# GpSimd subtracts for 17 units of the input projection, not 36; latent attention as two runs of four heads

## The chip, the cores and the metric

The kernel runs on one core of one Trainium2 chip. A core has five engines that work side by side, each through its own queue in order: TensorE (PE; its weight loads are shown as PEld), VectorE (DVE), ScalarE (ACT), GpSimd (POOL) and SyncE (SP, which issues the large loads). [...] The metric is the device time of one execution in microseconds (us); lower is better.

## The reference, cut to what matters

Two model blocks follow each other on 256 tokens of width 1024, in float32. The first block has a retention layer and a latent-attention layer, each with a feed-forward network (FFN) behind it; the second has a token mixer with a wide input projection, and a mixture of experts. The two pieces that the change touches:

```python
# latent attention, 8 heads, query blocks of 128 (16 meta tokens stand before the 256)
q = (cq @ w_q_b).reshape(B, L, 8, 128 + 64)
for qb in range(L // 128):
    sc = einsum('bqhd,bkhd->bhqk', q[:, s:e], k[:, :e]);  p = softmax(where(mask, sc, -1e30))
    outs.append(einsum('bhqk,bkhd->bqhd', p, v[:, :e]))
h = h + concat(outs) @ w_o                       # all heads

# token mixer of the second block
h = rms_norm(x, norm1_w) * (1 + sc1) + sh1
proj = h @ w_in                                   # 1024 x 5640: qa, ka, va, qkv_b, z, b, a, gates
```

## The kernel before, in words

Activations lie transposed, features on 128 partitions and tokens along the row. A float32 product is made of three products of fp32r operands: every weight and every activation x is cut into a high part `hi` (ACT rounds x to fp32r, L162) and a low part `lo` = x - hi (L168), and `mm3` (L306) issues hi·xh, hi·xl and lo·xh into one PSUM bank.

Weights come in chunks of 16 tiles of 128x128 (1 MB) that SP loads ahead into 5 buffers; a **unit** is 8 tiles, 128x1024, and is cut by one ACT and one subtraction. `Weights.ahead` (L151) keeps three units cut ahead of the products, in 4 buffers of `hi` and 4 of `lo`. The subtraction of a unit is written one unit later than its `hi`. `W.aside` (L257) names the units whose subtraction is put on GpSimd instead of DVE: here the 36 units from the first one that holds tiles of `win`, the input projection of the token mixer. That first unit, number 0 in this text, holds the last four tiles of the FFN's second product and the first four of `win`.

The order of the work is the order in which the Python code runs; nothing reorders it. `gemm` (L362) walks through column groups, each of two PSUM banks, and calls `tick` after every tile; every fourth (or ninth) tick takes one step of each generator in `sides` (L330): small work that is threaded between the products. `evac` reads a finished bank. `later` keeps small DVE instructions for the next ticks. `drain` and `until` take side steps with no products between them.

**Latent attention** (L817 to L951). `mla_proj(g)` makes keys, values and queries of heads 4g to 4g+3. It ends with two column groups that give `qn`, two heads each. The heads go through `pipeline` (L918): `scores` (two heads at a time on PE; mask, softmax on DVE and ACT), a free step, `trans` (five transposes on PE, copies `pt` and `ptm` on ACT) and `av` (four products on PE, then `oh`, `ol` by ACT and DVE, shown as `xbh`, `xbl`). At each time t the pipeline takes av of head t-3, trans of t-2 and scores of t. One pipeline walks through all 8 heads, and scores of heads 4 to 7 are let in when `ready` is set, after all of `mla_proj(1)`. Then `until` (L940) steps on until four heads are out, `mo` multiplies them by the first half of w_o, `drain` ends the other four, and `mo` takes the second half.

**The input projection** (L973 to L1480). The FFN of the first block ends with `evac_f1` (L958): hx is added up (L937), ACT makes the square, the scaled x and `xbh`, DVE makes `xbl` and two sums of squares. Products: `ba` (8 tiles), `qa2` and `ka2` (32 each, on xbh/xbl, 258 columns), then `va2` (32, weights moving), `dn` (96), `z` (32), the gates `ga`, `gb`. While ba, qa2 and ka2 run, DVE and ACT make the eight row blocks of the normed input (`modulated`, L1000: L1004, L1005 on DVE, L1006 on ACT, L1008 on DVE), read out qm and km (L1139), and prepare decays (`decays`, L1071; its cols at L1091 go into a small PE product at L1096). `va2` is not begun before `modulated` is through (L1164). `lev` (L1039) and the bias tables (`m_bias`, L1153) are loaded from GpSimd's queue.

Of the kernel before, what the change touches and what calls it, by code (L numbers as in the profile page):

```python
# [18 lines left out]
SEQ = 256  # L19
# [220 lines left out]
def body(ctx, tc, I, O):  # L240
    nc = tc.nc
    V, A, P = nc.vector, nc.scalar, nc.tensor
# [11 lines left out]

    W = Weights(nc, rawp, splitp, I["wd"], I["we"], order, split, 5, 4)
    first_win = min(i for i, t in enumerate(order) if t and t[0] == "win") // UNIT
    W.aside = lambda v: first_win <= v < first_win + 36  # L257

    hx = keep.tile([128, KD, T], F32, name="hx")
    vec = const.tile([128, VEC["n"]], F32, name="vec")  # L260
# [37 lines left out]
    def bank(pool, name):  # L298
        return pool.tile([128, 512], F32, tag=name, name=name)
# [6 lines left out]
    def mm3(ps, w, x, first, last):  # L306
        P.matmul(ps, w[0], x[0], start=first, stop=False)  # L307
        P.matmul(ps, w[0], x[1], start=False, stop=False)  # L308
        P.matmul(ps, w[1], x[0], start=False, stop=last)  # L309

    def mm3t(ps, x, w, first, last):
        P.matmul(ps, x[0], w[0], start=first, stop=False)
        P.matmul(ps, x[0], w[1], start=False, stop=False)
        P.matmul(ps, x[1], w[0], start=False, stop=last)

    def split_to(hi, lo, src):
        A.activation(hi, src, AF.Copy)  # L317
        V.tensor_sub(lo, src, hi.bitcast(F32))  # L318
# [9 lines left out]
    sides = []  # L328

    def side_step():  # L330
        for g in list(sides):
            try:
                next(g)
            except StopIteration:
                sides.remove(g)

    def drain(gen):
        while gen in sides:
            side_step()

    def until(done):
        while not done():
            side_step()
# [7 lines left out]
    def flush():  # L351
        while pend:
            pend.pop(0)()

    def tick(every=4):
        quantum[0] += 1
        if pend and quantum[0] % 2 == 0:
            pend.pop(0)()
        if quantum[0] % every == 0:
            side_step()  # L360

    def gemm(mat, ks, ngroups, g, x, n, evac, after_first=None, every=4, hold=False):  # L362

        for gi in range(ngroups):
            pss = [bank(mmp, "mm") for _ in range(g)]
            for kk in range(ks):
                for j in range(g):
                    mm3(pss[j][:, :n], W.take(mat), x(kk), kk == 0, kk == ks - 1)
                    tick(every)
            flush()  # L370
            if gi == 0 and after_first:
                after_first()
                if not hold:
                    flush()
            for j in range(g):
                evac(gi * g + j, pss[j][:, :n])
        if not hold:
            flush()
# [71 lines left out]
    o = VEC["mix0"][0]  # L450
# [39 lines left out]
    def rope(put, pss, cs, n):  # L490

        c, s = cs[:, 0], cs[:, 1]
        for j, (a, b, op) in enumerate(((c, s, OP.subtract), (s, c, OP.add))):
            def half(j=j, a=a, b=b, op=op):
                t = tmp.tile([128, 2, T], F32, tag="rt", name="rt")
                V.tensor_mul(t[:, 0, :n], pss[0], a)
                V.tensor_mul(t[:, 1, :n], pss[1], b)
                put(j, op, t[:, 0, :n], t[:, 1, :n])
            later(half)
# [160 lines left out]
    def ffn_open(which):  # L660
        return dict(x=xbuf(which), acc=keep.tile([128, T], F32, tag="acc", name="facc"))
# [57 lines left out]
    la = {}  # L719
# [85 lines left out]
    G = {}  # L805

    def normq():
        r = la["rq"] = row_scale(qacc, SEQ, 1.0 / 768, 1e-6, "rq", lat)
        V.tensor_scalar(r, r, 192.0 ** -0.5, None, op0=OP.mult)
        cs = la["qcs"] = lat.tile([128, 2, SEQ], F32, name="qcs")  # L810
        for j in range(2):
            V.tensor_mul(cs[:, j], rope_m[:, j], r)

    cpair = lambda k: (ch[:, k], cl[:, k])
    qpair = lambda k: (qh[:, k, :SEQ], ql[:, k, :SEQ])

    def mla_proj(g):  # L817
        d = G[g] = {}
        kn = d["kn"] = pb.tile([128, 4, T], F32, tag="kn", name="kn")
        gemm("kvb", 4, 2, 2, cpair, T,  # L820
             lambda j, ps: V.tensor_mul(kn[:, j], ps, la["rc"]))
        pss = [bank(mmp, "mm") for _ in range(2)]
        pm = bank(sdp, "side")
        i = W.pos
        for k in range(4):
            w = W.take("kvb", 4)
            for j in range(2):
                o = 128 * j
                mm3t(pss[j], (ch[:, k, o:o + 128], cl[:, k, o:o + 128]), w, k == 0, k == 3)
                tick()  # L830
        for k in range(4):
            P.matmul(pm[32 * k:32 * k + 32], c32[:, k], W.raw_at(i + 4 * k, 4), start=True, stop=True,
                     tile_position=(0, 32 * k))
        v = d["v"] = pb.tile([128, 2, 512], F32, tag="lv", name="lv")
        for j in range(2):
            A.activation(v[:, j], pss[j], AF.Copy, scale=la["rccol"][:, j:j + 1])
        mp = lat.tile([128, 512], F32, tag="lmp", name="lmp")
        A.activation(mp, pm, AF.Copy)
        if g == 0:
            normq()  # L840
        qr = d["qr"] = pb.tile([128, 2, SEQ], F32, tag="qr", name="qr")
        got = []

        def put(i, op, a, b):

            for h in range(4):
                o = 64 * (h % 2) + 32 * i
                V.tensor_tensor(qr[o:o + 32, h // 2], a[32 * h:32 * h + 32], b[32 * h:32 * h + 32], op=op)

        def evac(j, ps):  # L850
            got.append(ps)
            if j == 1:
                rope(put, got, la["qcs"], SEQ)
        gemm("qb", 6, 1, 2, qpair, SEQ, evac)
        pv = bank(sdp, "side")
        P.matmul(pv[0:16], gsel, mp, start=True, stop=True)
        vm = d["vm"] = pb.tile([16, 512], F32, tag="lvm", name="lvm")
        A.activation(vm, pv[0:16], AF.Copy)
        qn = d["qn"] = pb.tile([128, 4, SEQ], F32, tag="qn", name="qn")
        gemm("qb", 6, 2, 2, qpair, SEQ, lambda j, ps: V.tensor_mul(qn[:, j], ps, la["rq"]))  # L860
        d["ready"] = True

    H = {}

# [41 lines left out]
    def av(h):  # L906
        g, i = divmod(h, 4)
        d, e = G[g], H.pop(h)
        c = slice(128 * i, 128 * i + 128)
        po = bank(sdp, "side")  # L910
        P.matmul(po[:, 0:256], d["v"][:, 0, c], e["t"][:, 0:256], start=True, stop=False)
        P.matmul(po[:, 128:256], d["v"][:, 1, c], e["t"][:, 256:384], start=False, stop=False)
        P.matmul(po[:, 64:128], d["v"][0:16, 1, c], e["tm"][:, 64:128], start=False, stop=False)
        P.matmul(po[:, 192:256], d["vm"][:, c], e["tm"][:, 192:256], start=False, stop=True)
        split_to(oh[:, h], ol[:, h], po[:, 0:256])
        la["heads"] = h + 1

    def pipeline(stages, n, ready=None, lead=0):  # L918
        m = len(stages)
        for t in range(n + m - 1):  # L920
            if t == 2:
                for _ in range(lead):
                    yield
            for si in reversed(range(m)):
                if 0 <= t - si < n and stages[si]:
                    while ready and not ready(si, t - si):
                        yield
                    stages[si](t - si)
                    yield

    mla_proj(0)
    mside = pipeline([scores, None, trans, av], 8, lambda si, h: si or "ready" in G.get(h // 4, {}))
    sides.append(mside)
    mla_proj(1)

    def add_x(j, ps):
        V.tensor_add(hx[:, j, XS], hx[:, j, XS], ps)  # L937

    opair = lambda k: (oh[:, k], ol[:, k])
    until(lambda: la.get("heads", 0) >= 4)  # L940
    gemm("mo", 4, 4, 2, opair, SEQ, add_x)
    drain(mside)
    F1 = ffn_open("a")

    def evac_l1(j, ps):
# [8 lines left out]
    o = VEC["fin"][0]  # L954
# [1015 lines left out]
    g = [st[:, 3, t:t + 1] for t in range(2)]  # L1970
# [150 lines left out]
```

## Time and profile before

| what | value |
|---|---|
| time, median of 3 runs | 1294.42 us (1292.28 to 1295.43) |
| the profiled execution: its own time, its span | 1295.5 us, 1293.7 us |
| PE busy | 1223.9 us, 95% |
| DVE, ACT, POOL busy | 799.5, 597.4, 99.9 us |
| mean granted TensorE clock | 0.973 |
| latent attention, projections to the last head | about 450 to 579 us |
| ba to va2 | 778 to 840 us |
| dn, z, ga, gb | 840 to about 955 us |

How to read it: matmuls overlap each other, so a busy PE is an upper bound, and PE is waiting only where a row names idle time before an instruction. [...] Idle time on the other engines costs nothing by itself. From about 1050 us on the expert weights come in at some 415 GB/s; SP starts to issue them when the token mixer's buffers are given up.

### The profile page before, as it was taken

Reading aid. Unit: us, or ns where it says so; the run is one execution under the profiler, and the core shown is the slowest. Engines: PE = TensorE matmul, PEld = TensorE weight load, DVE = VectorE, ACT = ScalarE, POOL = GpSimd, SP = SyncE. Lnnn points to the kernel's source line nnn. Section 1 sums busy time; section 2 is a strip of 40 time slices with the busy share of each in tenths; the row PEclk is TensorE's granted clock in tenths of the full one; section 3 lists DMA queues with packets and bytes.
Section 4 is the critical chain, followed back from the end, with each engine's and each line's share of the span. In section 5 each row is a group of like instructions: output and inputs, shape, how many; then the busy total and the mean of one; then the engine's idle time right before and its main releaser. Section 6 shows DMA issues by size and latency. Waiting matters only on the chain. (4 is left out here: it accounts for less than half of the span.)

```text
span 1293.7 us, 24265 instructions
## 1 busy us (share of the span) xinstructions
PE 1223.9 (95%) x9994; PEld 1055.7 (82%) x9994; DVE 799.5 (62%) x1404; ACT 597.4 (46%) x1017; POOL 99.9 (8%) x59
## 2 busy tenths in 40 slices
PE   8999999999999999999999998799999998777896
PEld 7889798999999998889999998599789974232453
DVE  7465665987777887649877887646645743121223
ACT  5544546644445564556544554667334531010123
POOL 0000000000000000000000025667100000000000
PEclk9999999999999999989999998899999999897898
DMA  8433434476657854414766784444114779999992
GB/s 299 177 144 130 144 126 175 152 264 225 228 193 296 314 176 183 164 66 166 291 228 233 271 296 157 151 158 164 67 67 176 317 288 414 417 418 418 417 418 76
DMA packets 47362, 293.08 MB, mean 227 GB/s; under 512 B 6384, under 2 KB 7296, under 8 KB 15360
## 3 DMA queue, kind: packets, MB, share of 16 engines
q1 hardware_dynamic: 45216, 286.52, 58.5%
q0 software_dynamic: 2016, 4.76, 1.0%
q8 instruction: 90, 1.47, 0.5%
q14 instruction: 40, 0.33, 0.1%
HBM read 290.19 MB, written 3.16 MB: 227 GB/s over the span
## 5 line engine op out<-in xcount | busy, mean ns | idle before, releaser
L162 ACT ACTIVATE hi<-raw 128x1024 fp32r<-128x1024 f32 x295 | 309.1, 1052 | 156.9 <-PE mm L308 115.4
L168 DVE TENSOR_TENSOR lo<-raw,hi 128x1024 fp32r<-128x1024 f32 x259 | 315.3, 1227 | 15.3 <-ACT hi L162 15.0
L307 PE MATMUL mm<-xah,hi 128*128 128x256 f32 (+1 forms) x1040 | 304.6, 293 | 1.2 <-ACT hi L179 1.2
L309 PE MATMUL mm<-xah,lo 128*128 128x256 f32 (+1 forms) x1040 | 293.5, 282 | 2.1 <-DVE lo L168 1.9
L308 PE MATMUL mm<-xal,hi 128*128 128x256 f32 (+1 forms) x1040 | 293.4, 282 | 0.1
L307 PEld LDWEIGHTS mm<-xah,hi 128*128 128x128 f32 x1040 | 195.5, 188 | 18.7 <-issue 9.6
L309 PEld LDWEIGHTS mm<-xah,lo 128*128 128x128 f32 x1040 | 195.5, 188 | 3.2 <-DVE lo L168 2.5
L308 PEld LDWEIGHTS mm<-xal,hi 128*128 128x128 f32 x1040 | 195.7, 188 | 0.7 <-DVE xal L322 0.3
L307 PE MATMUL mm<-xbh,hi 128*128 128x272 f32 (+2 forms) x600 | 173.8, 290 | 3.4 <-ACT xbh L644 3.3
L309 PE MATMUL mm<-xbh,lo 128*128 128x272 f32 (+2 forms) x600 | 172.7, 288 | 1.9 <-POOL lo L168 1.9
L308 PE MATMUL mm<-xbl,hi 128*128 128x272 f32 (+2 forms) x600 | 173.4, 289 | 0.0
L307 PEld LDWEIGHTS mm<-xbh,hi 128*128 128x128 f32 x600 | 115.0, 192 | 5.7 <-ACT xbh L644 3.9
L309 PEld LDWEIGHTS mm<-xbh,lo 128*128 128x128 f32 x600 | 114.6, 191 | 2.1 <-POOL lo L168 2.1
L168 POOL TENSOR_TENSOR lo<-raw,hi 128x1024 fp32r<-128x1024 f32 x36 | 89.0, 2488 | 344.8 <-ACT hi L162 341.7
L308 PEld LDWEIGHTS mm<-xbl,hi 128*128 128x128 f32 x600 | 114.5, 191 | 0.6 <-DVE xbl L645 0.5
L307 PE MATMUL mm<-hh,hi 128*128 128x272 f32 (+1 forms) x352 | 100.3, 285 | 0.0
L308 PE MATMUL mm<-hl,hi 128*128 128x272 f32 (+1 forms) x352 | 100.2, 285 | 0.0
L309 PE MATMUL mm<-hh,lo 128*128 128x272 f32 (+1 forms) x352 | 99.9, 284 | 0.0
L1755 PE MATMUL side<-raw,xg 128*32 128x512 f32 x512 | 68.8, 654 | 19.2 <-DMA raw<-we 15.4
L1755 PEld LDWEIGHTS side<-raw,xg 128*32 128x32 f32 x512 | 15.5, 113 | 64.2 <-DMA raw<-we 33.7
L309 PEld LDWEIGHTS mm<-hh,lo 128*128 128x128 f32 x352 | 66.4, 189 | 0.0
L308 PEld LDWEIGHTS mm<-hl,hi 128*128 128x128 f32 x352 | 66.4, 189 | 0.0
(550 smaller groups left out, 1901.0 us busy)
## 6 DMA issues: line engine op xcount, KB each, us to landing
raw<-wd SPq DMA_DIRECT2D x171, 1024.0 KB, 4.8
raw<-we SPq DMA_DIRECT2D x78, 1024.0 KB, 15.9
spare<-we SPq DMA_DIRECT2D x12, 512.0 KB, 16.0
half<-we SPq DMA_DIRECT2D x12, 512.0 KB, 13.4
big<-we SPq DMA_DIRECT2D x6, 512.0 KB, 18.8
pot<-we SPq DMA_DIRECT2D x6, 512.0 KB, 17.6
e<-e POOLq DMA_DIRECT2D x1, 2048.0 KB, 19.4
bias<-e POOLq DMA_DIRECT2D x8, 192.0 KB, 2.9
```

Source lines behind the costliest of these rows:

```text
L162: self.nc.scalar.activation(hi, w, AF.Copy)
L168: (self.nc.gpsimd if self.aside(v) else self.nc.vector).tensor_sub(lo, w, hi.bitcast(F32))
L307: P.matmul(ps, w[0], x[0], start=first, stop=False)
L308: P.matmul(ps, w[0], x[1], start=False, stop=False)
L309: P.matmul(ps, w[1], x[0], start=False, stop=last)
L1755: P.matmul(ps[32 * i:32 * i + 32], x[:, 32 * i:32 * i + 32], w(512 * i, 512), start=k == 0, stop=k == KD - 1, tile_position=(0, 32 * i))
```

## The change

Two independent edits. `W.aside` now names units 14 to 30 (17 units) instead of 0 to 35: the subtractions of units 0 to 13 and 31 to 35 are put on DVE. And the eight heads go through two pipelines of four: the first ends by itself while `mla_proj(1)` runs, the second is taken up as soon as the first two of its heads have `qn` (after the first of the two column groups); `until` becomes `drain(mside[0])`. No instruction is added or left out.

```diff
-    W.aside = lambda v: first_win <= v < first_win + 36
+    W.aside = lambda v: first_win + 14 <= v < first_win + 31
...
-        gemm("qb", 6, 2, 2, qpair, SEQ, lambda j, ps: V.tensor_mul(qn[:, j], ps, la["rq"]))
-        d["ready"] = True
+
+        def put_q(j, ps):
+            V.tensor_mul(qn[:, j], ps, la["rq"])
+            d["ready"] = j + 1
+            if g and j == 1:
+                sides.append(mside[1])
+
+        gemm("qb", 6, 2, 2, qpair, SEQ, put_q)
...
         split_to(oh[:, h], ol[:, h], po[:, 0:256])
-        la["heads"] = h + 1
...
+    def heads(o):
+
+        stages = [f and (lambda h, f=f: f(o + h)) for f in (scores, None, trans, av)]
+        return pipeline(stages, 4, lambda si, h: si or G[o // 4].get("ready", 0) > h)
+
+    mside = [heads(0), heads(4)]
     mla_proj(0)
-    mside = pipeline([scores, None, trans, av], 8, lambda si, h: si or "ready" in G.get(h // 4, {}))
-    sides.append(mside)
+    sides.append(mside[0])
     mla_proj(1)
...
-    until(lambda: la.get("heads", 0) >= 4)
+    drain(mside[0])
     gemm("mo", 4, 4, 2, opair, SEQ, add_x)
-    drain(mside)
+    drain(mside[1])
```

ACT at the end of `mla_proj(1)`, from `lvm` (the values of the meta tokens) on. `hi` is a weight unit, the lines on `sc,st` are the softmax of a head, `pt` and `ptm` are the copies behind `trans`, `xbh` the high part of a finished head. Before:

```order
L858 ACTIVATE lvm<-side 16x512
L162 ACTIVATE hi<-raw 128x1024 x3
L887 ACTIVATE sc,st<-sc,st 128x144
L887 ACTIVATE sc,st<-sc,st 128x272
L890 ACTIVATE sc<-sc,st 128x144
L890 ACTIVATE sc<-sc,st 128x272
L317 ACTIVATE xbh<-side 128x256
L903 ACTIVATE pt<-side 128x384
L904 ACTIVATE ptm<-side 16x256
```

and in the changed kernel, the same stretch:

```order
L858 ACTIVATE lvm<-side 16x512
L317 ACTIVATE xbh<-side 128x256
L162 ACTIVATE hi<-raw 128x1024
L909 ACTIVATE pt<-side 128x384
L910 ACTIVATE ptm<-side 16x256
L317 ACTIVATE xbh<-side 128x256
L162 ACTIVATE hi<-raw 128x1024
L893 ACTIVATE sc,st<-sc,st 128x144
L893 ACTIVATE sc,st<-sc,st 128x272
```

The last `pt` of the first four heads stood behind the softmax of head 4, with no weight unit between; now it stands two weight units earlier, ahead of that softmax.

DVE where the FFN ends, up to the addition of its last two blocks (`hx<-hx,mm`); L410, L415 and L418 belong to the modulation vector of the second block. Before:

```order
L410 ISA junk,mod<-raw,crow 128x1024
L410 ISA mod 128x1
L168 TENSOR_TENSOR lo<-raw,hi 128x1024
L410 ISA junk,mod<-raw,crow 128x1024
L410 ISA mod 128x1
L415 TENSOR_TENSOR mod<-mod,vec 128x24
L418 SCALAR_TENSOR_TENSOR a_126<-mod,vec 128x8
L937 TENSOR_TENSOR hx<-hx,mm 128x256 x2
```

and in the changed kernel (its line 947 is line 937 of before):

```order
L410 ISA junk,mod<-raw,crow 128x1024
L410 ISA mod 128x1
L168 TENSOR_TENSOR lo<-raw,hi 128x1024 x2
L410 ISA junk,mod<-raw,crow 128x1024
L410 ISA mod 128x1
L415 TENSOR_TENSOR mod<-mod,vec 128x24
L418 SCALAR_TENSOR_TENSOR a_126<-mod,vec 128x8
L168 TENSOR_TENSOR lo<-raw,hi 128x1024 x2
L947 TENSOR_TENSOR hx<-hx,mm 128x256 x2
```

The subtractions of units 0, 1 and 2, which were GpSimd's, stand on DVE ahead of that addition.

DVE at the end of `ka2`: the last blocks of `modulated`, and the cols that PE's product at L1096 waits for (L1091, now L1101). Before:

```order
L1139 TENSOR_TENSOR km<-mm,rr 128x256 x2
L1008 TENSOR_TENSOR xal<-gt,xah 128x256
L1004 TENSOR_TENSOR gt<-hx,rr 128x256
L1005 TENSOR_SCALAR gt<-gt,a_125,mod 128x256
L1008 TENSOR_TENSOR xal<-gt,xah 128x256
L1004 TENSOR_TENSOR gt<-hx,rr 128x256
L1005 TENSOR_SCALAR gt<-gt,a_125,mod 128x256
L1090 SCALAR_TENSOR_TENSOR cols<-cols 128x8
L1091 SCALAR_TENSOR_TENSOR cols<-cols,ea 128x8
```

and in the changed kernel:

```order
L168 TENSOR_TENSOR lo<-raw,hi 128x1024
L1149 TENSOR_TENSOR km<-mm,rr 128x256 x2
L1018 TENSOR_TENSOR xal<-gt,xah 128x256
L1014 TENSOR_TENSOR gt<-hx,rr 128x256
L1015 TENSOR_SCALAR gt<-gt,a_125,mod 128x256
L168 TENSOR_TENSOR lo<-raw,hi 128x1024 x2
L1018 TENSOR_TENSOR xal<-gt,xah 128x256
L1014 TENSOR_TENSOR gt<-hx,rr 128x256
L1015 TENSOR_SCALAR gt<-gt,a_125,mod 128x256
L1100 SCALAR_TENSOR_TENSOR cols<-cols 128x8
L1101 SCALAR_TENSOR_TENSOR cols<-cols,ea 128x8
```

Three subtractions stand in this piece, units 9 to 11; from the reciprocal of the norm (L997) to these cols there are eight (units 4 to 11), where before there were none. Further on, five more (units 31 to 35) stand between DVE's steps of the delta rule (L1273 to L1357).

## Rows read from the trace of the kernel before

**Rows 1.** The page: PE's busy time; its granted clock in 40 slices.
```profile
PE 1223.9 (95%) x9994; PEld 1055.7 (82%) x9994; DVE 799.5 (62%) x1404; ACT 597.4 (46%) x1017; POOL 99.9 (8%) x59
PEclk9999999999999999989999998899999999897898
```

**Rows 2.** PE's waits: line, what it waited for, us in total, times, longest.
```profile
PE side L1096 <- DVE cols L1091: 5.2, 1, 5.2
PE mm L307 <- ACT xbh L644: 3.3, 1, 3.3
...
PE mm L309 <- POOL lo L168: 1.9, 1, 1.9
...
PE side L1350 <- DVE X L1302: 1.8, 1, 1.8
...
PE side L1184 <- ACT stb L1179: 1.2, 1, 1.2
```

**Rows 3.** Windows: stretch, its length, busy us of PE, PEld, DVE, ACT, POOL; PEclk, DMA.
```profile
551.70:558.50 6.80, 6.28 (x26) 5.61 (x26) 3.29 (x7) 2.88 (x11) 0.00 (x0) 0.50 0.00 0
...
769.40:778.00 8.60, 8.60 (x75) 8.60 (x74) 8.56 (x6) 3.18 (x3) 8.56 (x3) 1.00 0.76 251
...
783.80:790.60 6.80, 6.73 (x23) 5.58 (x24) 4.15 (x8) 3.91 (x6) 2.43 (x1) 0.50 0.16 39
...
814.50:824.80 10.30, 5.07 (x21) 3.71 (x21) 9.71 (x10) 3.86 (x8) 8.08 (x7) 0.50 0.51 173
```

**Rows 4.** Timeline of PE: start, us, instruction, idle before it and its releaser.
```profile
552.22 0.80 PE L911 MATMUL side<-pt,lv 128*128 128x256 f32 x1 [1.64 <-ACT pt L903]
...
778.09 0.28 PE L307 MATMUL mm<-xbh,hi 128*128 128x258 f32 x1
...
780.12 0.28 PE L309 MATMUL mm<-xbh,lo 128*128 128x258 f32 x1
783.73 0.55 PE L307 MATMUL mm<-xbh,hi 128*128 128x258 f32 x1 [3.33 <-ACT xbh L644]
...
787.59 0.78 PE L307 MATMUL mm<-xbh,hi 128*128 128x258 f32 x1
...
821.40 0.39 PE L1096 MATMUL side<-cols,lev 64*64 64x8 f32 x4 [5.23 <-DVE cols L1091]
```

**Rows 5.** Timeline of all engines at the stall in latent attention.
```profile
548.48 0.59 DVE L884 TENSOR_TENSOR sc<-side,mmask 128x416 f32<-128x416 f32 x1 [2.28 <-PE side L879]
...
550.69 0.83 ACT L890 ACTIVATE sc<-sc,st 128x144 f32<-128x144 f32 x2 [0.23 <-DVE st L888]
...
551.69 0.48 ACT L903 ACTIVATE pt<-side 128x384 f32<-128x384 f32 x1
```

**Rows 6.** Timeline of DVE from the end of the FFN to ba's readout.
```profile
769.82 3.42 DVE L168 TENSOR_TENSOR lo<-raw,hi 128x1024 fp32r<-128x1024 f32 x1
...
778.93 2.89 DVE L418 SCALAR_TENSOR_TENSOR a<-mod,vec 128x8 f32<-128x8 f32 x1
781.74 0.74 DVE L937 TENSOR_TENSOR hx<-hx,mm 128x256 f32<-128x256 f32 x2
...
788.69 1.75 DVE L997 RECIPROCAL rr<-rr 128x256 f32<-128x256 f32 x1 [2.37 <-ACT rr L996]
790.55 0.42 DVE L1123 TENSOR_TENSOR ga<-mm,rr 128x256 f32<-128x256 f32 x1
```

**Rows 7.** Timeline of ACT: the first weight unit behind ba's readout.
```profile
793.14 1.04 ACT L162 ACTIVATE hi<-raw 128x1024 fp32r<-128x1024 f32 x1
```

**Rows 8.** Single lines: instructions, ns of one (least, median, most), first and last start.
```profile
L168 DVE TENSOR_TENSOR lo<-raw,hi x259: 1175/1219/3424, 13.8 to 1042.4; 128x1024 fp32r<-128x1024 f32 x130
...
L168 POOL TENSOR_TENSOR lo<-raw,hi x36: 2348/2405/3385, 769.4 to 915.0; 128x1024 fp32r<-128x1024 f32 x36
...
L1008 DVE TENSOR_TENSOR xal<-gt,xah x8: 417/1228/3960, 794.5 to 827.2; 128x256 fp32r<-128x256 f32 x8
...
L1005 DVE TENSOR_SCALAR gt<-gt,a,mod x8: 411/414/415, 791.3 to 826.3; 128x256 f32<-128x256 f32 x8
```

## The prediction, made before the changed kernel was run

> **What bounds the kernel now.** The page's first two parts are read first: PE is busy 95% of the span, the granted clock is whole but for a few slices [rows 1]. So what the change can give lies in PE's idle time and in stretches at half its clock, and is looked for there. PE's waits come second: three stand around ba, qa2 and ka2 (3.3 us for `xbh`, 1.9 for a GpSimd `lo`, 5.2 for DVE's cols) [rows 2], and PE's timeline has one of 1.64 for `pt` in latent attention [rows 4]. [...]
>
> Fourth, why DVE and ACT were late. In latent attention `pt` of head 3 starts at 551.69, right behind the softmax scaling of head 4 (550.69, two of 0.83 together) [rows 5]; that is order on ACT alone. Around 770 to 825 it is DVE: one `lo` is 3.42 us where the median is 1.22, a sum of 8 columns is 2.89, L1008 goes from 0.42 to 3.96 [rows 6, 8]. From 769.4 to 778.0 GpSimd is busy all 8.56 us with three subtractions, and DVE, busy as long, finishes about one instruction for each [rows 3]. L1005 beside them, with one tensor from SBUF, is never over 0.415 us [rows 8]. So a DVE instruction with two inputs in SBUF waits while a GpSimd subtraction (2.4 us) runs. The last addition of the FFN, whose products end at 778.09, starts at 781.74 [rows 4, 6].
>
> [...]
>
> **The change part by part.** The sum is made against the profiled execution, 1295.5 us with a span of 1293.7; it lies at the upper end of the three runs, 1.1 above their median.
>
> *Latent attention.* The same PE work is written in another order. Gone is the 1.64 us stall, and with it the half clock: from 552.2 to 558.5 PE works 6.3 us at half speed, worth 3.1 [rows 3, 4]. What is late next? The scores of head 4 now stand an av and twelve products behind the first two `qn`. 18 products take 2.15 us (778.09 to 780.12, and one more), 0.12 each [rows 4], so twelve take 1.43; from the av's end on, ACT must copy `xbh` and DVE write `xbl` and two `qn`, some 1.6 (0.4, 0.4 and twice 0.4): a stall of about 0.2. The transposes of head 4 stand 24 products, 2.9 us, behind its scores, whose softmax took 3.1 from DVE's first step (548.48) to the end of the scaling, 551.5 [rows 5], and a handover of 0.1 on either side: 0.3 to 0.4. An av stands twelve products behind its transposes, 1.43 us against 0.85 for the copies: nothing. Taken: 1.6 + 3.1 - 0.5 = 4.2 us gained. Bounds: 4.7, and 0 if one of the new waits grows to 1.6 and brings the half clock back.
>
> *The end of the FFN.* DVE gets units 0 to 2 ahead of L937, but nothing is stretched: from 769.9 it has three `lo` and two modulation steps at about 1.15 each, and is free at about 776, before the products end. L937 starts at 778.0, not 781.74. From it to the first product of qa2 it took 5.85 us (787.59), at half clock; at whole clock the two float32 sums between lose some 0.75. So qa2 starts at 783.1: 4.5 earlier [rows 4, 6]. PE's idle time there falls from 3.3 to about 1.2, in three pieces, and I take it that the clock stays up: 787.59 to 790.6 at half speed was worth 1.5 [rows 3]. If it falls all the same, PE is 3 later, but see below.
>
> *qa2 and ka2.* PE's span from 787.59 to the stall's begin at 816.17 is 28.6. Without the 1.9 us wait and the half clock (1.5, and 0.8 from 814.5 on) it is 24.4: PE comes to L1096 at 807.5 [rows 2 to 4]. DVE has to be there with L1091. It starts its reciprocal when L937's chain and a table load are through, at 784.3 (before: 788.69, less the 3.7 of L937 and 0.7 of clock) [rows 6]. Up to L1091: reciprocal 1.75, ba's readout 0.42, seven modulated blocks at 1.25, three pairs of readouts at 0.75, small columns 0.6, and the eight new `lo` at 1.22, 9.8: 23.6. Successive rows overlap by some 0.08 (778.93 + 2.89 against 781.74), over 40 instructions 3 us: 20.5. Waits for ACT: the next `hi` ends 3.6 us behind ba's readout (790.55 to 794.18) [rows 6, 7], with 2.2 of work to fill it, 1.4; another table load of that kind 1.0; the tanh and the last `hi` 1.1. Together 24 to 25: L1096 at 809.4, not 821.4, and a stall of 2 us where 5.2 were. All `lo` are there when PE asks: unit 9's about 1.5 us ahead. Gained: 12.0. Bounds for L1091, which has no such row before: as PE arrives, 807.5 (and no half clock after it); or half of the stretched time stays, 815.
>
> *va2.* Before, it held 3.4 us at half clock after 821.4 (1.7) and a stall of 1.2 [rows 2, 3]. Behind a 2 us stall the clock probably falls: 6.8 at half, 3.4 lost, while PE's slowness gives the softmax time and the 1.2 go. Taken: 0.5 lost. If the clock fell at 784 instead, PE comes later, waits less here and loses no clock here; the two cases end within a microsecond.
>
> *dn to the gates.* Units 14 to 30 stay on GpSimd. Units 31 to 35 stand on DVE in the delta rule, ahead of L1302, for which PE waits 1.8 [rows 2]. Of three `lo` one falls into DVE's idle time, so 2.4 us come on top; in return no GpSimd subtraction holds a DVE step there, each for up to 2.4 [rows 8], and there were three. I take 0.7 gained; bounds -2.4 and 1.8.
>
> Later, SP loads by what PE has freed, so a shift is kept to the end. Sum: 4.2 + 12.0 - 0.5 + 0.7 = 16.4, 1279.1 for the profiled execution; for waits too small to list I take 1 us off: 1280, against a median of 1294.4.
>
> **The rivals.** *The half clock comes back in latent attention* (12%). For it: one of the two new waits need only be 1.6, as the old one was, and ACT has a weight unit of 1.04 to do beside each softmax [rows 5, 7]. Against it: products now stand between all the small groups. The rest alone is left: 1295.5 - 12.2 + 1 = 1284.
>
> *DVE is fuller than I count* (17%). For it: 24 us of work and waits in a stretch of 24, with ACT waiting for DVE and DVE for ACT in turn. L1091 then comes at 813 to 815, PE stalls 5 us or more and runs at half clock after it: 4 to 5 us less, 1285.
>
> *DVE becomes the bound, and the kernel slower* (6%). Place: the queue from the reciprocal to L1091. If the long rows came from something other than GpSimd, it keeps its 32.5 us (788.7 to 821.2) and gets eight `lo` of 1.15, 9.2, on top; L1096 is at 830.6, and the FFN's end is as late as before. With latent attention's 4.2: 1295.5 + 9.2 - 4.2 = 1300.5. It decides from 37 us on for that queue, where nothing of the projection's gain is left, and 41 for a slower kernel. Against it: L1005 unstretched among stretched neighbours.
>
> *The projection gains, but va2 or the delta rule gives it back* (6%): two `lo` between the first softmaxes of va2, five in the delta rule, each 1.2 on a path PE waits for, and a lasting half clock: 8 us, 1288.
>
> **How the numbers follow.** The forecast, 1276 to 1283.5, has 59%. What a measurement of this kernel can tell is about 0.3%, 3.9 us: faster is below 1290.5. All cases but the DVE-bound one lie there, though a share of the last rival and of what I have not seen does not: faster 0.88, same 0.05, slower 0.07. The range takes in the two rivals at 1284 and 1285 and the better bounds (no stall at L1096, no half clock: 1274.5): 1275 to 1287.
>
> **What would show it.** Right: no DVE row over 1.3 us among `lo`, L1004 and L1008 before dn; L937 at the end of the FFN right behind the last product; PE's waits for `pt` and for GpSimd's `lo` gone; the half clock from 552 gone; L1096 still waiting for L1091, about 2 us. Wrong: long rows on DVE with GpSimd idle; a stall over 4 us at L1096; a new half-clock stretch between 536 and 580; PE waiting for DVE's `lo` in qa2 or ka2.

## The result, and the profile after

The changed kernel takes 1277.29 us (median of four runs, 1276.47 to 1277.64) against 1294.14 for the kernel before (four runs, 1292.28 to 1295.43). The ratio is 0.9867, with a 95% interval of 0.9855 to 0.9879: 17 us, or 1.3%, faster. The prediction said 1280, with a range of 1275 to 1287. The profiled execution took 1277.64 us, with a span of 1275.8. (In the changed kernel line numbers are 6 to 10 higher: L1096 is L1106, L1091 is L1101, L1350 is L1360, L937 is L947, L1008 is L1018, L911 is L917.)

The page first, PE's busy time and its granted clock in 40 slices, to be held against [rows 1]:

```profile
PE 1218.2 (95%) x9994; PEld 1051.6 (82%) x9994; DVE 787.6 (62%) x1423; ACT 597.9 (47%) x1017; POOL 51.4 (4%) x40
PEclk9999999999999999999999999999999999897998
```

GpSimd is down from 99.9 to 51.4 us, and DVE does 19 more instructions in 12 us less. That is the first thing to see: its added work was smaller than the stretching that went. The clock's row has lost its three slices below 9 ahead of the mixture of experts (MoE).

PE's waits from 530 to 1000 us (line, what it waited for, us in total, times, longest) answer to [rows 2]:

```profile
PE side L1106 <- DVE cols L1101: 1.6, 1, 1.6
PE side L1360 <- DVE X L1312: 0.8, 1, 0.8
PE mm L309 <- DVE lo L168: 0.8, 1, 0.8
PE side L882 <- DVE qn L862: 0.6, 1, 0.6
PE side L1307 <- DVE ns L1300: 0.4, 1, 0.4
PE side L917 <- ACT pt L909: 0.4, 1, 0.4
PE mm L307 <- ACT xbh L644: 0.4, 1, 0.4
```

The wait for `xbh` is down from 3.3 to 0.4, the one for GpSimd's `lo` is gone, the one for cols is down from 5.2 to 1.6. What is new is 0.6 for `qn`. PE's timeline (start, us, instruction, idle before it) at the places of [rows 4]:

```profile
554.74 0.39 PE L882 MATMUL side<-kn,qn 128*128 128x144 f32 x1 [0.59 <-DVE qn L862]
...
777.77 0.38 PE L307 MATMUL mm<-xbh,hi 128*128 128x258 f32 x1 [0.36 <-ACT xbh L644]
...
779.41 0.47 PE L307 MATMUL mm<-xbh,hi 128*128 128x258 f32 x1
...
805.38 0.28 PE L1106 MATMUL side<-cols,lev 64*64 64x8 f32 x4 [1.65 <-DVE cols L1101]
```

One stretch at half clock is left before the MoE, 3.4 us behind the stall at L1106; [rows 3] had three with 24 us. Each of those three began after PE had begun to stand still: 1.1 us after it in latent attention, 3.4 at the wait for `xbh`, and 2.4 at the 1.9 us wait for `lo`, which ended at 814.03 [rows 2 to 4]; this one begins 2.2 us after. The window (length, busy us of PE, PEld, DVE, ACT, POOL, clock, DMA share):

```profile
805.90:809.30 3.40, 3.40 (x12) 2.23 (x12) 1.59 (x5) 2.83 (x6) 0.00 (x0) 0.50 0.22 89
```

DVE's timeline, for [rows 6], shows where the time was: the last addition of the FFN is at 774.37 and waits for PE now, and from the reciprocal (780.49) to L1101 (805.15, 0.17) it is 24.8 us.

```profile
774.37 0.78 DVE L947 TENSOR_TENSOR hx<-hx,mm 128x256 f32<-128x256 f32 x2 [1.71 <-PE mm L309]
...
780.49 1.75 DVE L1007 RECIPROCAL rr<-rr 128x256 f32<-128x256 f32 x1 [0.38 <-ACT rr L1006]
...
805.15 0.17 DVE L1101 SCALAR_TENSOR_TENSOR cols<-cols,ea 128x8 f32<-128x8 f32 x1
```

And the single lines (ns: least, median, most), for [rows 8]: no `lo` over 1.23 us where one was 3.42, no L1018 over 0.43 where one was 3.96.

```profile
L168 DVE TENSOR_TENSOR lo<-raw,hi x278: 1175/1219/1227, 13.6 to 1023.8; 128x1024 fp32r<-128x1024 f32 x139
L1018 DVE TENSOR_TENSOR xal<-gt,xah x8: 414/418/425, 787.2 to 807.6; 128x256 fp32r<-128x256 f32 x8
L168 POOL TENSOR_TENSOR lo<-raw,hi x17: 2375/2400/2450, 818.3 to 870.6; 128x1024 fp32r<-128x1024 f32 x17
```

A ledger, made by setting PE's instructions at the same place of the program side by side: the two profiled executions differ by 0.14 us from the start on. Latent attention then gives 3.4. From there to L1096/L1106 (821.40 against 805.38) it is another 12.5, by the end of va2 1.7 more, by the delta rule 0.8 more: 18.4. The MoE gives 0.6 of it back.

### The profile page after: what moved, and what is told of

Same layout as the page of the kernel before. It is cut to its first block, busy times and chain, and to the rows that moved or that the text cites. A ratio compares the mean times of both kernels' runs of the same rounds, so it can differ in the third digit from the quotient of the medians.

```text
span 1275.8 us, 24246 instructions
## 1 busy us (share of the span) xinstructions
PE 1218.2 (95%) x9994; PEld 1051.6 (82%) x9994; DVE 787.6 (62%) x1423; ACT 597.9 (47%) x1017; POOL 51.4 (4%) x40
## 5 line engine op out<-in xcount | busy, mean ns | idle before, releaser
L168 DVE TENSOR_TENSOR lo<-raw,hi 128x1024 fp32r<-128x1024 f32 x278 | 336.2, 1218 | 20.3 <-ACT hi L162 20.0
L309 PE MATMUL mm<-hh,lo 128*128 128x272 f32 (+1 forms) x352 | 99.9, 284 | 0.0
L307 PEld LDWEIGHTS mm<-hh,hi 128*128 128x128 f32 x352 | 66.2, 188 | 0.0
```

Of the source, the lines that this page charges most:

```text
L168: (self.nc.gpsimd if self.aside(v) else self.nc.vector).tensor_sub(lo, w, hi.bitcast(F32))
```

## The experiments

All times are medians; the ratio is to the kernel before, run in the same session. That kernel's own medians were 1294.14 (with the changed kernel), 1295.63 (e1 to e4), 1294.56 (e5 to e7, q4) and 1295.96 us (e8, e9, q5), so the us of different sessions can't be compared to better than some 2 us; the ratio is an estimate over the runs and differs from the quotient of the medians by up to 0.0012 (q5). A short table, and then each run by itself.

| run | us | ratio | 95% interval |
|---|---|---|---|
| changed kernel | 1277.29 | 0.9867 | 0.9855 to 0.9879 |
| e1_heads: latent attention alone | 1293.04 | 0.9983 | 0.9973 to 0.9994 |
| e2_aside: GpSimd's share alone | 1278.72 | 0.9868 | 0.9852 to 0.9885 |
| e3_none: no unit on GpSimd | 1280.89 | 0.9885 | 0.9868 to 0.9901 |
| e4_first3: units 0 to 2 given back | 1277.65 | 0.9863 | 0.9847 to 0.9879 |
| e8_tail: units 31 to 35 given back | 1278.45 | 0.9870 | 0.9855 to 0.9885 |
| e5_twice: nine subtractions added | 1290.91 | 0.9974 | 0.9963 to 0.9984 |
| e6_once: nine copies added | 1282.10 | 0.9908 | 0.9892 to 0.9925 |
| e7_fill: before, stall filled with 14 | 1294.65 | 1.0000 | 0.9990 to 1.0009 |
| e9_fill7: before, stall filled with 7 | 1294.45 | 0.9986 | 0.9977 to 0.9995 |
| q4_later: L1106 two steps later | 1276.29 | 0.9868 | 0.9852 to 0.9885 |
| q5_both: and the transposes one later | 1274.65 | 0.9848 | 0.9834 to 0.9861 |

**Each part alone.** e1_heads is the changed kernel with this line as before:

```
-    W.aside = lambda v: first_win + 14 <= v < first_win + 31
+    W.aside = lambda v: first_win <= v < first_win + 36
```

> Only latent attention's two runs of four heads; GpSimd takes all 36 units, as before. Theory (the two parts save in places of their own): the 1.64 us stall and the 6.8 us of half clock behind it are gone, and 3.6 us are kept, as the changed kernel's ledger has at its last delta-sum of latent attention (602.41 against 598.84): 1290.5, ratio 0.997; the stalls at xbh (3.3), at the GpSimd lo (1.9) and at cols (5.2) stand as before. Rival (work that comes earlier only waits longer at the next stall): the wait at L1106 grows by the 3.6 us and the time stays at 1294, ratio 1.000.

Measured: 0.17% (0.06 to 0.27), 0.8 to 3.5 us. In the profiled execution 3.5 us are won in latent attention and kept to the delta rule, and PE's waits behind it are those of [rows 2] again (5.4 for cols, 3.3, 1.9, 1.8, 1.2). So the rival, that the gain only waits longer at L1106, is out; the time holds the expected 3.6 just outside its interval.

e2_aside is the kernel before, with the line of the changed kernel (the one with the minus) and nothing else.

> Only GpSimd's share is changed (units 14 to 30); latent attention as before, with its 1.64 us stall. Theory: FFN end to ka2 give 12.4, va2 1.6, the tail 0.9, less 0.6 given back later: 14 saved, 1280.5, ratio 0.989, and with the other part alone it adds up to the whole change. Rival (the two parts need each other, since the projection's vector work is late only with latent attention late): 8 or less saved, 1286 or more. If the range is worth less than the ledger says, a half-clock stretch or a wait at cols over 4 us stands here.

Measured: 1.32%, where both parts together have 1.33%. With e1's 0.17% the sum is 1.49%; the intervals are wide enough for the two to add up, but not to show it. The traces say more. Alone, this part gives 16.5 us up to the delta rule, and e1 3.5, 20.0 in all, against 18.4 for both. The 1.6 between are one thing: behind the same stall at cols (1.68 us here, 1.65 there) the clock fell in the changed kernel, 3.4 us at half, and did not fall here. Each trace is of one execution.

**What GpSimd's share does, place by place.** e3_none: `W.aside = lambda v: False`.

> The changed kernel with no low part on GpSimd at all: 17 more lo, 20.7 us of DVE at 1.22 each, in dn and the stage after it, where DVE is busy 27 of 53 us. Theory (what counts is the stretching of DVE's rows, and DVE has room there): 1276 to 1280, ratio to before 0.986 to 0.989. Rival (GpSimd's 17 are a relief that DVE needs, as a count of its busy time at 1.2 us a unit would say): 8 us or more lost, 1285 or more.

Measured 0.9885, some 2.3 us above the changed kernel by the ratios. The two intervals overlap, but all of its runs (1279.93 to 1281.33) lie above those of e4 in the same session (1276.50 to 1279.18). That is at the end of the theory's range, and its reason does not hold: in the trace 3.1 us are lost, all behind 840 us, where most of the 17 `lo` fall. PE's waits from 780 us on and the window:

```profile
PE side L1210 <- ACT stb L1197: 1.7, 3, 1.1
PE side L1106 <- DVE cols L1101: 1.6, 1, 1.6
...
809.00:862.00 53.00, 51.29 (x377) 44.85 (x374) 37.80 (x85) 36.10 (x87) 2.15 (x4) 1.00 0.39 135
```

DVE has room there (37.8 of 53 us busy), and a new wait for va2's probabilities stands there all the same: the low parts are in the queue ahead of softmax steps that come as a chain (the one for which PE waits 1.1 us starts on DVE at 847.34 here, behind two of them, and at 845.58 in the changed kernel). So here GpSimd is worth 2 to 3 us, though DVE has the room. The rival's size (8) was wrong, its direction right.

e4_first3: `first_win <= v < first_win + 3 or first_win + 14 <= v < first_win + 31`.

> The changed kernel with units 0 to 2 given back to GpSimd, the three that run beside the FFN's last products. Theory (the three subtractions stretch DVE's rows there, one for each): L947 starts late again by about 3.4 us, the wait for xbh is 3 us again, the clock falls behind it (6.8 us at half, of which qa2 holds some); a part of this is taken up by the 1.65 us wait at L1106: 1280 to 1283. Rival (the end of the FFN was late for another reason, and only units 3 to 13 matter): 1277, with the xbh wait as short as in the changed kernel.

Measured 0.9863, as the changed kernel. But the long rows are there. DVE's timeline, and GpSimd's below it:

```profile
766.82 3.42 DVE L168 TENSOR_TENSOR lo<-raw,hi 128x1024 fp32r<-128x1024 f32 x1
770.17 3.43 DVE L410 CUSTOM_DVE_ANT_0 junk<-raw,crow 128x1024 bf16<-128x1024 f32 x1
...
773.64 2.27 DVE L415 TENSOR_TENSOR mod<-mod,vec 128x24 f32<-128x24 f32 x1
775.93 0.17 DVE L418 SCALAR_TENSOR_TENSOR a<-mod,vec 128x8 f32<-128x8 f32 x1
```

```profile
766.36 9.49 POOL L168 TENSOR_TENSOR lo<-raw,hi 128x1024 fp32r<-128x1024 f32 x3 [289.94 <-ACT hi L162]
```

Three subtractions, three long rows: 6.5 us of stretch, where three `lo` of DVE's own are 3.7. Less what DVE had idle ahead of L947, PE comes to L1106 1.1 us later than in the changed kernel (both starts set equal). The theory's 3.4 was too much: it left out that DVE is spared three `lo` of 1.22. In the profiled execution nothing of it is left, since the clock did not fall behind L1106 here (the window below), and did there (1.7); the times alone could not show 1.1 us. Of the 12.5 us, these three units hold one; the rest is, by difference, the fourth subtraction and those behind it.

```profile
807.00:812.00 5.00, 4.98 (x30) 3.94 (x31) 3.50 (x12) 4.16 (x13) 0.54 (x1) 1.00 0.24 96
```

e8_tail: `first_win + 14 <= v < first_win + 36`.

> The changed kernel with units 31 to 35 given back to GpSimd, the ones that are cut in the delta rule. Theory (there a subtraction of GpSimd holds the two-input steps of DVE for which PE waits): the wait for X grows from 0.8 back to 1.8 us and 0.5 to 1 us is lost, 1278. Rival (DVE has no room there and the five were better on GpSimd): 1275 to 1276. Both are near what can be told apart in time; the wait at the X product in the trace decides.

Measured 0.9870 and, in the waits:

```profile
PE side L1360 <- DVE X L1312: 1.8, 1, 1.8
```

1.8 against 0.8, as the theory said; the time can't tell it, the wait does.

**Is it GpSimd that stretches DVE's rows?** e5_twice adds an instruction to GpSimd and nothing to DVE; the spare tile takes a place that is free until the delta rule.

```
+            self.twice(v, hi)
...
+    dump = sp.tile([128, UNIT * 128], F32, tag="t6", name="dump")
+    W.twice = lambda v, hi: first_win + 3 <= v < first_win + 12 and nc.gpsimd.tensor_sub(
+        dump, hi.bitcast(F32), hi.bitcast(F32))
```

> The changed kernel, in which GpSimd also does nine subtractions with two inputs in SBUF, one when each of units 3 to 11 is cut (2.35 us each, into a tile that nothing reads yet); DVE still does every lo itself, so its work and its order are those of the changed kernel. Theory (a DVE instruction with two SBUF inputs waits while such a GpSimd instruction runs): rows of DVE at L168, L1014, L1018 of 2.4 to 4 us again, up to one for each of the nine; the wait at L1106 grows from 1.65 to 6 to 10 us, and the time to 1282 to 1287. Rival (the long rows before came from the order of DVE's own work, or from DMA traffic): rows of 1.22 and 0.42, 1277.

Measured 1290.91, beyond the theory's range; by the ratio four fifths of the gain are lost. DVE's timeline beside two of the nine (lines are 2 to 4 higher here), GpSimd's, and PE's wait:

```profile
788.41 1.22 DVE L168 TENSOR_TENSOR lo<-raw,hi 128x1024 fp32r<-128x1024 f32 x1 [1.33 <-ACT hi L162]
789.56 2.12 DVE L1020 TENSOR_TENSOR xal<-gt,xah 128x256 fp32r<-128x256 f32 x1
791.60 2.11 DVE L1016 TENSOR_TENSOR gt<-hx,rr 128x256 f32<-128x256 f32 x1
793.74 0.41 DVE L1017 TENSOR_SCALAR gt<-gt,a,mod 128x256 f32<-128x256 f32 x1
```

```profile
788.52 4.90 POOL L1053 TENSOR_TENSOR dump<-hi 128x1024 f32<-128x1024 f32 x2 [7.65 <-ACT hi L162]
```

```profile
PE side L1110 <- DVE cols L1105: 8.9, 1, 8.9
```

GpSimd's two end at 791.39 and 793.42; DVE's two rows of 0.42 take 2.1 each and end 0.3 behind them. From 775 to 817.5 just nine rows of DVE are over their length in the changed kernel by more than 0.1, one for each of the nine, by 12.4 us in all, and L1110 (the old L1096) is 12.2 later, at 817.58, with a wait of 8.9. By the same count the kernel before had eleven such rows with 23.0 us up to L1091, and the changed kernel has none. L1017 with one tensor from SBUF stays at 0.41, and at 0.51 at most. The theory holds, with a larger price than I gave it: I had bounded it by a part of the nine, and it was all of them. (Of the profiled execution's time another 3 us are lost far behind, where the clock is at half for 6.8 us from 977.3 and PE waits for nothing that the profile shows; what set that off is open.) (The added instruction also holds each `hi` tile longer; PE's wait of 0.9 for a `lo` at 804 may come from that.)

e6_once puts `nc.gpsimd.tensor_copy(dump, hi.bitcast(F32))` in the same place, one input in place of two.

> As the run with nine more subtractions on GpSimd, but each is a copy of hi, with one input in SBUF. [...]

Measured 1282.10, with a ratio of 0.9908 where the changed kernel has 0.9867. DVE's timeline, GpSimd's, and PE's wait:

```profile
787.39 1.26 DVE L1020 TENSOR_TENSOR xal<-gt,xah 128x256 fp32r<-128x256 f32 x1
788.57 1.25 DVE L1016 TENSOR_TENSOR gt<-hx,rr 128x256 f32<-128x256 f32 x1
789.86 0.41 DVE L1017 TENSOR_SCALAR gt<-gt,a,mod 128x256 f32<-128x256 f32 x1
```

```profile
786.34 3.21 POOL L1053 COPY dump<-hi 128x1024 f32<-128x1024 f32 x2 [6.61 <-ACT hi L162]
```

```profile
PE side L1110 <- DVE cols L1105: 5.8, 1, 5.8
```

A copy does it too: GpSimd's instruction need not have two inputs. Seven rows are longer, by 4.5 us, and L1110 is 4.0 later: less than in e5, where a subtraction took 2.34 us in the mean and a copy here 1.43.

**Is half clock worth what it costs?** e7_fill is the kernel before with its 1.64 us stall filled:

```
+        if h == 3:
+            busy(14, bank(mmp, "mm"), ident)
         po = bank(sdp, "side")
```

> The kernel before, with 14 products of the identity into an unused bank put ahead of the product that stands still 1.64 us in latent attention (1.4 to 1.7 us of PE work in the idle time). Theory (the half clock from 551.7 on comes from the stall): the stretch at 0.50 after it is gone, the 6.8 us of half clock give back 3.1, 1291, ratio 0.9975. Rival (the half clock comes from something else, so that the stall alone was worth anything): the stretch at 0.50 stays, 1294 to 1295.

Measured 1.0000: nothing. The 14 products are 28 PE instructions in the trace and took 3.1 us (550.18 to 553.30), so PE came to the av 1.3 us late by my own doing. The windows, at the old stretch and at a new one:

```profile
551.70:558.50 6.80, 6.80 (x57) 6.52 (x56) 3.17 (x7) 4.27 (x12) 0.00 (x0) 1.00 0.01 2
982.30:985.70 3.40, 3.40 (x17) 3.40 (x17) 1.46 (x3) 2.41 (x6) 0.00 (x0) 0.50 0.10 19
```

The stretch at 551.7 is gone, as the theory says. But two of 3.4 us stand at 910.6 and 982.3, where the kernel before has none, and ahead of the second PE waits for nothing that the profile shows. The stretch that the kernel before has from 814.5 for 10.2 us is 13.7 long here, from 811.6. So I ran it again with `busy(7, ...)`:

> The kernel before with 7 products of the identity, not 14, ahead of the product that waits for pt: 14 filled 3.1 us where the stall was 1.64 and cost 1.3 us of their own; 7 take some 1.6 and no more than the stall. Theory (the half clock that follows the stall comes from the stall, and what is won there stays): the stretch at 0.50 from 551 on is gone and 3 us are kept, 1291.5, ratio 0.9977. Rival (half clock that is avoided at one place comes back at others, as the run with 14 had it at 910.6 and 982.3): the stretch at 551 is gone, new stretches stand later, and the time is 1294, ratio 1.000.

```profile
550.25 1.73 PE L304 MATMUL mm<-ident 128*128 128x128 f32 x14
552.05 0.70 PE L913 MATMUL side<-pt,lv 128*128 128x256 f32 x2
```

```profile
551.70:558.50 6.80, 6.73 (x50) 5.91 (x49) 3.24 (x7) 4.34 (x12) 0.00 (x0) 1.00 0.01 2
```

The filling takes as long as the stall, the clock stays up, and PE is 2.8 us ahead from there to the delta rule in the profiled execution, with no new stretch. In time it is 0.14% (0.05 to 0.23), 0.6 to 3.0 us: a gain, and at most the theory's 3. That the half clock there comes from the stall is shown; how much of what is won is given back in other executions is open, since only one of each was profiled.

**A better kernel.** q4_later moves the product that PE still waits for in the changed kernel:

```
     def decays(ga):
...
-        yield from pause(2)
+        yield from pause(4)
         ps = bank(sdp, "side")
         for p in range(2):
             rs = half_of(p)
             P.matmul(ps[rs, 0:8], lev[rs, 7], by_block(QE)[rs], start=True, stop=True, tile_position=(64 * p, 64 * p))
```

> The changed kernel, with the product at L1106 two steps of the side work later: it stands behind the first products of va2 and not ahead of them. Theory: the 1.65 us wait there and the 3.4 us of half clock behind it (1.7) are gone, and the eight columns are not needed until the delta rule: 3.3 saved, 1274. Rival (PE comes earlier to va2's transposes, whose softmax needs as long as before): a wait of 1 to 2 us for stb takes its place, with 1.7 saved at most: 1275.5 to 1277.

Measured 0.9868, not to be told from the changed kernel. The waits from 780 us on:

```profile
PE side L1194 <- ACT stb L1189: 1.6, 1, 1.6
```

The rival was right. The wait at L1106 and the half clock behind it are gone, PE comes to va2's first transposes earlier, and their softmax takes as long as it took. In the trace 1.3 us are left of 3.3. So q5_both keeps q4's edit and moves these as well, with one step of lead:

```
         A.activation(by_block(GS), ps[:, 0:8], AF.Copy)
-        yield from pause(2)
+        yield from pause(3)
...
-    mob = pipeline([m_scores, None, m_trans, m_av], 8, lambda si, h: si < 3 or "vm2" in B2, 0)
+    mob = pipeline([m_scores, None, m_trans, m_av], 8, lambda si, h: si < 3 or "vm2" in B2, 1)
```

> The changed kernel with three steps of side work moved: the product at L1106 two steps later, as before, the product at L1111 one more, and the first transposes of va2 one step later (six products of 512 columns, 1.5 us), for which PE waited 1.58 us at 810.4. Theory: no wait over 0.5 us between 780 and 880, 1.3 to 1.6 less than with L1106 alone, 1274.5 to 1275. Rival (cols or the second softmax is late in its turn, or the MoE's loads end when they did): 1276 to 1277.

```profile
PE side L1360 <- DVE X L1312: 0.8, 1, 0.8
PE side L1307 <- DVE ns L1300: 0.4, 1, 0.4
PE side L1194 <- ACT stb L1189: 0.2, 1, 0.2
```

Measured 1274.65, ratio 0.9848: as the theory said, with no wait over 0.5 us left between 780 and 880 and 2.7 us won in the trace against the changed kernel. Its interval (0.9834 to 0.9861) still touches the changed kernel's, so the 2.5 us between the two ratios are likely and not proved by the times; the trace is what speaks for them.

## Why the prediction was right

The time, its sign and its largest term came out as forecast, and by the mechanism named; the smaller terms were off, in both directions.

*GpSimd's subtractions hold DVE's two-input instructions.* Right, and shown by adding some (e5, e6). In e5 DVE's tensor-tensor rows of 0.42 us took 2.1 beside a GpSimd subtraction, and in e6 1.25 beside a GpSimd copy.

*End of the FFN, qa2 and ka2: 12.0 predicted, 12.5 measured.* The queue from the reciprocal to L1101 was to take 24 to 25 us and took 24.8. L1106 stands still 1.65 us; 2 were forecast. The first product of qa2 is at 779.41. In the kernel before it is at 787.59 [rows 4], 784.03 without the 3.56 by which PE was ahead already: 4.6 earlier, 4.5 forecast, with the clock up throughout. The row count above says why that sum could be made by hand: 23.0 us of stretch went, and twelve `lo` of 1.22 came (units 0 to 11, 14.6 us).

*Latent attention: 4.2 predicted, 3.4 measured in the trace, 0.8 to 3.5 in the time of e1.* The step that failed is "what is late next". I looked for the new wait at the scores and transposes of head 4 (0.2 and 0.3 to 0.4, taken as 0.5); both came without a wait worth listing, and 0.59 stand at 554.74, the scores of head 6, the first of the second pair of `qn`. The split into two runs makes each pair of `qn` a gate of its own, and I worked out one of the two. That 0.5 and 0.59 are alike is luck, since they are waits at different places. The half clock there was put at 3.1; e9, which takes away that alone, has 2.8, and 1.64 + 2.8 - 0.59 is 3.9; the 0.4 that is left I have not traced.

*va2: 0.5 lost predicted, 1.7 gained measured.* The step was that the clock falls for 6.8 us behind the stall. It fell for 3.4, so that as much half clock stands there as before, and the 1.2 for `stb` are gone; the other 0.5 are not traced. In e2, e4 and e8 it did not fall at all behind the same stall, and in e3 for 3.4 again, so this term could not be known better than to 1.7 us; the prediction gave it as a single number, and of the wrong sign.

*dn to the gates: 0.7 predicted, 0.8 measured*, and e8 has the wait for X go back to 1.8.

*Waits too small to list: 1 lost predicted, 0.6 given back in the MoE.* These are not the same thing, so the likeness says nothing for the term. The sum of the errors, 0.5 - 0.8 + 2.2 + 0.1 + 0.4, is the 2.4 us by which the profiled execution beat the 1280. That it is no more is in part luck: the short gain in latent attention set off a third of what va2 gave beyond its forecast.

Of the rivals none came. The one in which DVE becomes the bound had the long rows come from something else than GpSimd; e5 says they don't. The one in which DVE is fuller than counted needed a wait of 5 us at L1106.

## What to carry to other kernels

Work that is moved to an idle engine is not free if that engine holds up the one that it relieves: count for each moved instruction how long the other engine's rows become while it runs (here about one row of DVE for each instruction of GpSimd, up to 2.7 us longer in the eleven counted and 3.5 in the L1008 of 3.96 behind them, against 1.22 us saved), and give GpSimd its work where nobody waits for DVE's two-input steps. Read the stretching from rows of one line at its least and its most, and not from the busy share, which counts the waiting as work. When a stall goes, name what is late next at every gate of the new order, and look whether the next one can be moved too: q4 without q5 gave nothing that could be measured.

## What the runs showed of the hardware that was not expected

In e5 a DVE instruction with two SBUF inputs that began while one of GpSimd's added subtractions ran was held until that ended, however short it is itself: all nine long rows end within 0.3 us behind the end of one of them, and the second step on cols, of 128x8, took 1.02 us in e5 and 0.17 in the changed kernel:

```profile
797.82 1.02 DVE L1098 SCALAR_TENSOR_TENSOR cols<-cols 128x8 f32<-128x8 f32 x1
```

GpSimd's instruction need not have two inputs: beside two of its copies, 3.21 us together, DVE's rows of 0.42 took 1.26 and 1.25 (e6). And it goes both ways: GpSimd's added subtractions in e5 take 1.89 to 1.96 us in five cases, and 2.83 to 2.87 in the four that begin beside a `lo` of DVE.

The clock's fall behind a stall is not the same every time. Behind 1.64 to 1.68 us at the same product it fell for 3.4 us in the changed kernel and in e3, and not at all in e2, e4 and e8; behind 1.81 to 1.84 us at X it fell in e7 and e8, and not in the kernel before, e1 and e9. In e7 it was at half for 3.4 us from 982.3 and in e5 for 6.8 from 977.3, by the records with PE busy all the while and without a wait in the 15 us before. What sets this was not tried.
